# First stage of a decoder trunk: all low halves of the weights on VectorE, and the residual as one VectorE pass per tile

## The chip, the cores and the metric

The kernel runs on one core of a Trainium2 chip. The core has TensorE (PE, matmuls into PSUM), VectorE (DVE), ScalarE (ACT) and GpSimd (POOL), and queues of DMA transfers that SyncE (SP), ScalarE and GpSimd issue. The metric is the device time of one execution in microseconds, lower is better. Line numbers L... are those of the kernel before, except where a text speaks of the changed kernel.

## The reference

One decoder layer over 512 tokens of width 1024. What the change touches is at its start: the input LayerNorm, the projection to `v`, and the residual.

```python
x = layer_norm(x, ln_in_g, ln_in_b)
...
z = jnp.einsum('bsd,de->bse', x, w_in) + b_in
u_a, v_a, x_b, gate_b, q_c, merge = jnp.split(z, SPLIT_POINTS, axis=-1)
o_a = spatial_gating(jax.nn.gelu(u_a), jax.nn.gelu(v_a), ln_v_g, ln_v_b, w_s, b_s)
...
x = layer_norm(ALPHA * x + m, ln1_g[l], ln1_b[l])
f = hierarchical_moe(x, ...)
x = layer_norm(ALPHA * x + f, ln2_g[l], ln2_b[l])
```

`spatial_gating` normalises `v`, mixes the 128 positions of each chunk by a causal matrix for each of 8 channel groups, and multiplies by `u`. `m` is the mixer's output, which ends in `+ b_o`.

## The kernel before, in words

**Precision.** Each float32 matrix that goes into a matmul is split into a high half, rounded to the matmul's type by a cast, and a low half, the source minus the high half. A product is three matmul passes: high times high, and the two mixed ones. The helper `split` (L81) does the cast on ScalarE and the subtraction on VectorE. Inside the stage for `v`, the helper `split_w` (L290) does it for the weights, and takes the engine of the subtraction as an argument.

**Tiles.** The 512 tokens are four tiles `xts_[0]` to `xts_[3]` of 128x1024, called x0 to x3 here (in the order of instructions they are x_103 to x_106). The weights for `v` are four loads `raws[0]` to `raws[3]`, each split in two pieces of 128x1024, so `split_w` is called eight times. Five of these subtract on GpSimd (pieces (0,0), (1,0), (2,0), (2,1), (3,0)), three on VectorE.

**The stage for v.** For each token tile t: LayerNorm in place on VectorE (statistics, a scalar-tensor pass with the mean, a chain of eight operations on one column for the reciprocal root, L124 to L135, and a second scalar-tensor pass, L158), eight transposes on TensorE into two PSUM tiles `aux`, and their split: four casts on ScalarE and four subtractions on VectorE (L82, L83, `hl<-aux`, 128x256 each). The cast of the second half of an `aux` tile waits for the subtraction of the first half. Then two outputs of 24 matmuls of 512 columns, called p00, p01, p10 ... p31 after tile and half. `vsplit` (L327) puts the transposes of the next token tile behind the eighth matmul of the second output. `vout` (L304) adds the bias on VectorE and applies GELU on ScalarE, and `vnorm` (L309) normalises a `v` tile on VectorE.

**The residual.** `residual(t)` (L318) turns a token tile into ALPHA * x + b_o: in place, one ScalarE pass and one GpSimd addition. A DMA on GpSimd's queue stores it to `xr_d`, which is read some 500 us later.

**The u loop** (L390) follows: four steps of two channels each. A channel is 24 matmuls for `u` (`ztile`, L199), GELU, four matmuls that mix `v` by the masked matrix `wst` (L403), and the gating on VectorE (L406, L410), whose product is split again. The weights of a step are one load `raw` of 1 MB, split in two pieces (L82 and L83, `hl<-raw`). The two buffers of these loads are first those of `raws[2]` and `raws[3]`: the load for the first step waits until both subtractions of `raws[2]` are done.

**What sets the order.** Each engine works through its queue in order. Inside the stage for `v` (between `man.enter_context` and `man.close()`) the order is that of the code. What lies behind, the u loop among it, is placed by a scheduler of the framework, which can lift instructions into gaps of that order: so the first u weights' split, the small operations on `lt` (L545 to L559), and the eight passes on `bs` (L388) come between instructions of the stage.

Of the kernel before, what the change touches and what calls it, by code (L numbers as in the profile page):

```python
# [9 lines left out]
F32 = mybir.dt.float32  # L10
# [3 lines left out]
AF = mybir.ActivationFunctionType  # L14
ALU = mybir.AluOpType
# [21 lines left out]
ALPHA = 2.0 ** 0.25  # L37
# [16 lines left out]
def trunk(ctx, tc, x, mem, rows, cols, wz, wkv, pac, pb8, pb2, wax, ws, wo, wr, br, we, out):  # L54
    nc = tc.nc
    pe, dve, act, pool, sp = nc.tensor, nc.vector, nc.scalar, nc.gpsimd, nc.sync
# [12 lines left out]
    def mmps():  # L69
        return psm.tile([P, 512], F32, name="mm")  # L70
# [4 lines left out]
    def bcast(eng, pool_, r, name):  # L75
        t = pool_.tile([P, D], F32, name=name)
        i = ROWS.index(r)
        eng.dma_start(t, rows[i:i + 1, :].to_broadcast([P, D]))
        return t

    def split(hi, lo, src):  # L81
        act.copy(hi, src)  # L82
        dve.tensor_tensor(lo, src, hi.bitcast(F32), op=ALU.subtract)  # L83
# [76 lines left out]
    def layer_norm(dst, src, g, b, eps=EPS):  # L160
        ln_end(dst, ln_begin(dst, src, g), b, eps)
# [7 lines left out]
    def cc(i):  # L169
        return col[:, i:i + 1]  # L170
# [77 lines left out]
    with ExitStack() as st_a:  # L248
# [35 lines left out]
        bo = bcast(sp, s0, "b_o", "bo")  # L284
# [2 lines left out]
        sp.dma_start(wst, ws)  # L287
        wv = {}

        def split_w(i, h, eng):  # L290
            t_ = (op_ if i < 2 else hlp).tile([P, 2, 2, 512], F32R, name="o" if i < 2 else "hl")
            src = raws[i][:, 2 * h:2 * h + 2, :]
            act.copy(t_[:, 0], src)  # L293
            eng.tensor_tensor(t_[:, 1], src, t_[:, 0].bitcast(F32), op=ALU.subtract)
            wv[i, h] = t_

        def vmm(t, n, ps, lo, hi):
# [15 lines left out]
        def vfull(t, n):  # L313
            ps = mmps()
            vmm(t, n, ps, 0, 24)
            return ps

        def residual(t):  # L318
            xr = xts_[t]
            act.activation(xr, xr, AF.Copy, scale=ALPHA)  # L320
            pool.tensor_tensor(xr, xr, bo, op=ALU.add)
            pool.dma_start(xr_d[t * P:(t + 1) * P, :], xr)

        def transx(t):
            transpose_split(xts_[t], dsth(t, 0), dsth(t, 1))

        def vsplit(t, n, next_t):  # L327
# [10 lines left out]
                                                         op0=ALU.subtract, op1=ALU.mult) for c in x0h])  # L338
        for c in x0h:
            dve.scalar_tensor_tensor(xts_[0][:, c], xts_[0][:, c], rstd, bi[:, c], op0=ALU.mult, op1=ALU.add)  # L340
        split_w(0, 0, pool)
        transx(0)
        split_w(0, 1, dve)
        split_w(1, 0, pool)
        split_w(1, 1, dve)
        p00 = vfull(0, 0)
        layer_norm(xts_[1], xts_[1], gi, bi)
        split_w(2, 0, pool)
        split_w(2, 1, pool)
        split_w(3, 0, pool)  # L350
        split_w(3, 1, dve)
        p01 = vsplit(0, 1, 1)
        pool.affine_select(wst, wst, pattern=[[0, 8], [1, P]], compare_op=ALU.is_ge, fill=0.0,
                           base=0, channel_multiplier=-1)
# [2 lines left out]
        vout(0, 1, p01)  # L357
        p10 = vfull(1, 0)
        ln_end(xts_[2], ln, bi)
        residual(0)  # L360
        p11 = vsplit(1, 1, 2)
        vout(1, 0, p10)
        ln = ln_begin(xts_[3], xts_[3], gi)
        vout(1, 1, p11)
        p20 = vfull(2, 0)
        ln_end(xts_[3], ln, bi)
        residual(1)
        p21 = vsplit(2, 1, 3)
        vnorm(0)
        vout(2, 0, p20)  # L370
        p30 = vfull(3, 0)
        vout(2, 1, p21)
        vnorm(1)
        residual(2)
        p31 = vfull(3, 1)
        vout(3, 0, p30)
        residual(3)
        vnorm(2)
        last = [vout(3, 1, p31), vnorm(NT - 1)]
        man.close()  # L380
# [1 line left out]
        for i in range(2):  # L382
# [3 lines left out]
            for g in range(4 * i, 4 * i + 4):  # L386
                bg = bs[:, g * P:(g + 1) * P]
                dve.scalar_tensor_tensor(bg, ps[:, (g % 4) * P:(g % 4 + 1) * P], cc(C_VB + g), bg,  # L388
                                         op0=ALU.mult, op1=ALU.add)
        for d2 in range(4):  # L390
            with ExitStack() as after:
                for i in last if d2 else ():
                    after.enter_context(tc.issue_after(i.ins))
                w = zunit(256)
            for c in range(2):
                g = 2 * d2 + c
                ps = mmps()
                ztile(ps, w, c)
                u = sa.tile([P, T], F32, name="u", bufs=2)
                act.activation(u, ps, AF.Gelu_apprx_tanh, bias=cc(C_U + g))  # L400
                pv = auxps()
                for ch in range(NT):
                    pe.matmul(pv[:, ch * P:(ch + 1) * P], lhsT=v[:, ch, g * P:(g + 1) * P],  # L403
                              rhs=wst[:, g, :], start=True, stop=True)
                s = sa.tile([P, T], F32, name="s", bufs=2)
                dve.scalar_tensor_tensor(s.rearrange("p (c t) -> p c t", t=P),  # L406
                                         pv.rearrange("p (c t) -> p c t", t=P), cc(C_VG + g),
                                         bs[:, None, g * P:(g + 1) * P].to_broadcast([P, NT, P]),
                                         op0=ALU.mult, op1=ALU.add)
                dve.tensor_tensor(s, s, u, op=ALU.mult)  # L410
                split(oa(0, g), oa(1, g), s)

    y[0] = yp.tile([P, KD, T], F32, name="y")

# [5 lines left out]
    with ExitStack() as sc_stack:  # L420
# [15 lines left out]
        for h in range(CH):  # L436
# [19 lines left out]
            for et in range(2):  # L456
# [5 lines left out]
                                         op0=ALU.add, op1=ALU.subtract)  # L462
# [3 lines left out]
            for tp in range(2):  # L466
                ps = auxps()
                for t in (2 * tp, 2 * tp + 1):
                    for et in range(2):
# [6 lines left out]
                                  op0=ALU.mult)  # L476
# [87 lines left out]
    with tc.tile_pool(name="sb", bufs=1, reuse_waits="tile") as sb:  # L564
        ob = o_tiles()
        for hp in range(NH // 2):
# [4 lines left out]
            for c in range(2):  # L571
                h = 2 * hp + c
# [4 lines left out]
                                  op0=ALU.mult, op1=ALU.add)  # L577
# [22 lines left out]
            for c in range(2):  # L600
                h = 2 * hp + c
# [629 lines left out]
    for b in range(nb):  # L1231
# [65 lines left out]
        h = gate_h(pu, gw, c)  # L1297
# [51 lines left out]
    h = gate_h(pu, gw, c)  # L1349
# [73 lines left out]
    with tc.If(n_extra > 0):  # L1423
# [4 lines left out]
        for j in range(NEXTRA):  # L1428
# [14 lines left out]
            h = gate_h(up_mm(b), blk["gwx"], col_)  # L1443
# [80 lines left out]
```

## Time and profile before

| | us |
|---|---|
| runs shown | 942.83, 945.6, 1786.38; median 945.6 |
| the profiled execution | 940.93 |
| its span | 939.1 |
| TensorE busy | 880.2 (94%) |
| VectorE busy | 600.0 (64%) |
| ScalarE busy | 452.8 (48%) |
| GpSimd busy | 116.0 (12%) |

The stage for `v` and the first channel of the u loop lie in the first 92 us of the span. A timeline's row has the start, the duration (of a merged row: from the first start to the last end), the engine, the line, the operation, the tiles written and read, the shapes and the count; in brackets stands how long the engine idled ahead of it, and what ended that. [...]

### The profile page before, as it was taken

Reading aid. Unit: us, or ns where it says so; the run is one execution under the profiler, and the core shown is the slowest. Engines: PE = TensorE matmul, PEld = TensorE weight load, DVE = VectorE, ACT = ScalarE, POOL = GpSimd, SP = SyncE. Lnnn points to the kernel's source line nnn. Section 1 sums busy time; section 2 is a strip of 40 time slices with the busy share of each in tenths; the row PEclk is TensorE's granted clock in tenths of the full one; section 3 lists DMA queues with packets and bytes.
Section 4 is the critical chain, followed back from the end, with each engine's and each line's share of the span. In section 5 each row is a group of like instructions: output and inputs, shape, how many; then the busy total and the mean of one; then the engine's idle time right before and its main releaser. Section 6 shows DMA issues by size and latency. Waiting matters only on the chain. (4 is left out here: it accounts for less than half of the span.)

```text
span 939.1 us, 11191 instructions
## 1 busy us (share of the span) xinstructions
PE 880.2 (94%) x4260; PEld 733.2 (78%) x4260; DVE 600.0 (64%) x1011; ACT 452.8 (48%) x632; POOL 116.0 (12%) x95
## 2 busy tenths in 40 slices
PE   4798999999999999999999999999998889999990
PEld 3686888889988888888878888788877678888880
DVE  6988546324545543335667856666189987689966
ACT  4333342224434442223696686633124656678851
POOL 4322000000000100000000000000000123233843
PEclk9898999999999999999999999999999999999995
DMA  9406222332323333212214322238663888799573
GB/s 344 175 23 226 88 90 91 111 112 95 130 90 127 125 134 112 90 57 101 90 57 146 113 77 100 92 101 312 282 244 138 274 317 283 245 295 401 166 181 106
DMA packets 29867, 148.88 MB, mean 159 GB/s; under 512 B 5538, under 2 KB 5794, under 8 KB 16497
## 3 DMA queue, kind: packets, MB, share of 16 engines
q1 hardware_dynamic: 21312, 128.81, 37.6%
q0 software_dynamic: 7056, 17.12, 7.0%
q10 hardware_dynamic: 1440, 2.19, 0.7%
q8 instruction: 35, 0.57, 0.3%
q14 instruction: 24, 0.19, 0.1%
HBM read 138.33 MB, written 18.35 MB: 167 GB/s over the span
## 5 line engine op out<-in xcount | busy, mean ns | idle before, releaser
L109 PE MATMUL mm<-hl 128*128 128x512 f32 x1440 | 336.2, 392 | 0.0
L109 PEld LDWEIGHTS mm<-hl 128*128 128x128 f32 x1440 | 270.9, 189 | 56.3 <-DVE bnst L114 0.2
L83 DVE TENSOR_TENSOR hl<-raw,hl 128x1024 fp32r<-128x1024 f32 (+1 forms) x117 | 137.7, 1181 | 135.3 <-ACT hl L82 134.7
L82 ACT CAST hl<-raw 128x1024 fp32r<-128x1024 f32 (+1 forms) x117 | 117.6, 1015 | 133.0 <-PE mm L109 121.2
L109 PE MATMUL mm<-o,hl 128*128 128x512 f32 x624 | 142.9, 389 | 1.1 <-ACT o L82 1.1
L109 PEld LDWEIGHTS mm<-o,hl 128*128 128x128 f32 x624 | 117.0, 188 | 25.8 <-ACT o L82 1.5
L109 PE MATMUL mm<-hl,xs 128*128 128x512 f32 x432 | 107.5, 404 | 0.5 <-DVE xs L83 0.5
L109 PEld LDWEIGHTS mm<-hl,xs 128*128 128x128 f32 x432 | 81.0, 191 | 19.5 <-DVE xs L83 1.1
L691 DVE TENSOR_TENSOR hl<-o,hl 128x1024 fp32r<-128x1024 f32 (+1 forms) x52 | 57.8, 1143 | 2.6 <-ACT hl L685 2.6
L1142 PE MATMUL mm<-hl,hT 128*128 128x512 f32 x196 | 50.6, 404 | 0.6 <-DVE hT L83 0.6
L1006 POOL DMA_INDIRECT xg<-x_d,ixg x1 | 1.1, 1089 | 400.9 <-DVE rtl L1065 400.9
L685 ACT CAST hl<-o 128x1024 fp32r<-128x1024 f32 x48 | 48.0, 1051 | 1.7 <-PE mm L1142 1.7
L1142 PEld LDWEIGHTS mm<-hl,hT 128*128 128x128 f32 x196 | 35.6, 189 | 8.4 <-DVE hT L83 1.1
L222 ACT ACTIVATE gate<-mm,col 128x512 f32<-128x512 f32 x24 | 16.5, 688 | 39.7 <-PE mm L109 39.6
L1131 DVE TENSOR_TENSOR hl<-raw,hl 128x1024 fp32r<-128x1024 f32 x26 | 30.7, 1223 | 4.3 <-PE mm L109 2.0
L1122 ACT CAST hl<-raw 128x1024 fp32r<-128x1024 f32 x32 | 31.9, 1050 | 0.0
L525 POOL MEMSET zero<- 128x1024 f32 x1 | 1.0, 953 | 240.9 <-PE mm L109 240.9
L301 PE MATMUL mm<-o,hl 128*128 128x512 f32 x96 | 26.1, 432 | 1.8 <-ACT o L293 1.8
L109 PE MATMUL mm<-memT,hl 128*128 128x256 f32 x192 | 27.3, 286 | 0.2 <-ACT memT L82 0.2
L109 PE MATMUL mm<-hl,yh 128*128 128x512 f32 x96 | 27.0, 429 | 0.0
L733 ACT COPY x1T<-aux 128x512 f32<-128x512 f32 x8 | 4.7, 587 | 44.0 <-PE aux L732 24.0
L109 PEld LDWEIGHTS mm<-memT,hl 128*128 128x128 f32 x192 | 24.9, 191 | 0.9 <-ACT memT L82 0.4
(325 smaller groups left out, 1200.6 us busy)
## 6 DMA issues: line engine op xcount, KB each, us to landing
raw<-in_wz_dram SPq DMA_DIRECT2D x32, 1024.0 KB, 4.8
o<-in_we_dram SPq DMA_DIRECT2D x24, 1024.0 KB, 7.2
raw<-in_we_dram SPq DMA_DIRECT2D x16, 1024.0 KB, 6.8
raw<-in_pac_dram SPq DMA_DIRECT2D x8, 1024.0 KB, 4.7
raw<-in_wkv_dram SPq DMA_DIRECT2D x8, 1024.0 KB, 4.8
rawx<-in_we_dram SPq DMA_DIRECT2D x8, 1024.0 KB, 5.4
raw<-in_pb_dram SPq DMA_DIRECT2D x4, 1024.0 KB, 4.9
raw<-in_wo_dram SPq DMA_DIRECT2D x4, 1024.0 KB, 4.8
```

What stands on the lines that cost most here:

```text
L82: act.copy(hi, src)
L83: dve.tensor_tensor(lo, src, hi.bitcast(F32), op=ALU.subtract)
L109: pe.matmul(ps, lhsT=a(sa_), rhs=b(sb_), start=first and i == 0, stop=last and i == 2)
L222: act.activation(store[j], ps, AF.Sigmoid, bias=cc(C_M + br_i * 8 + j))
L301: pe.matmul(ps, lhsT=xT(k, slice(t * P, (t + 1) * P))(sx), rhs=wv[2 * n + k // 4, k // 2 % 2][:, sw, k % 2, :], start=i == 0, stop=i == 23)
L685: act.copy(t[:, 0], raws[key, i // 2][:, (i % 2) * 1024:(i % 2 + 1) * 1024])
L691: (eng or dve).tensor_tensor(t[:, 1, c0:c1], src[:, c0:c1], t[:, 0, c0:c1].bitcast(F32), op=ALU.subtract)
L733: act.copy(x1T.rearrange("p k n -> p (k n)"), ps)
L1006: pool.indirect_dma_start(out=xg, out_offset=None, in_=x1_d[:, :], in_offset=bass.IndirectOffsetOnAxis(ap=ix[:, b:b + 1], axis=0), bounds_ ...
L1122: act.copy(dnh[key][:, :, n * 512:(n + 1) * 512], dn_half(key, n))
L1131: eng.tensor_tensor(dnl[key][n], dn_half(key, n), dnh[key][:, :, ns].bitcast(F32), op=ALU.subtract)
L1142: pe.matmul(ps, lhsT=hT[:, sa_, f, :], rhs=dn[sb_][:, f, :], start=i + f == 0, stop=i + f == 3)
```

## The change

`split_w` loses its engine argument and calls `split`, so all eight low halves of the weights are subtracted on VectorE. `residual(t)` becomes one scalar-tensor pass on VectorE (x * ALPHA + b_o, in place, 128x1024); the store stays on GpSimd's queue. The four calls of `residual` leave the stage for `v`, and stand behind the second channel of each step of the u loop in the code.

```diff
-        def split_w(i, h, eng):
+        def split_w(i, h):
             t_ = (op_ if i < 2 else hlp).tile([P, 2, 2, 512], F32R, name="o" if i < 2 else "hl")
             src = raws[i][:, 2 * h:2 * h + 2, :]
-            act.copy(t_[:, 0], src)
-            eng.tensor_tensor(t_[:, 1], src, t_[:, 0].bitcast(F32), op=ALU.subtract)
+            split(t_[:, 0], t_[:, 1], src)
             wv[i, h] = t_
...
         def residual(t):
             xr = xts_[t]
-            act.activation(xr, xr, AF.Copy, scale=ALPHA)
-            pool.tensor_tensor(xr, xr, bo, op=ALU.add)
+            dve.scalar_tensor_tensor(xr, xr, ALPHA, bo, op0=ALU.mult, op1=ALU.add)
             pool.dma_start(xr_d[t * P:(t + 1) * P, :], xr)
...
-        split_w(0, 0, pool)
+        split_w(0, 0)
         transx(0)
-        split_w(0, 1, dve)
-        split_w(1, 0, pool)
-        split_w(1, 1, dve)
+        split_w(0, 1)
+        split_w(1, 0)
+        split_w(1, 1)
         p00 = vfull(0, 0)
         layer_norm(xts_[1], xts_[1], gi, bi)
-        split_w(2, 0, pool)
-        split_w(2, 1, pool)
-        split_w(3, 0, pool)
-        split_w(3, 1, dve)
+        split_w(2, 0)
+        split_w(2, 1)
+        split_w(3, 0)
+        split_w(3, 1)
...
         ln_end(xts_[2], ln, bi)
-        residual(0)
...
-        residual(1)
...
-        residual(2)
...
-        residual(3)
...
                 split(oa(0, g), oa(1, g), s)
+            residual(d2)
```

The order of VectorE's queue at three places follows; `x_103` is x0, `x_104` x1, `x_105` x2. First, from the last passes of x0's LayerNorm to the low halves of `raws[0]` and `raws[1]` (`o`), before:

```order
L135 SCALAR_TENSOR_TENSOR lnr_147<-lnt_148,lnr_147 128x1
L340 SCALAR_TENSOR_TENSOR x_103<-x_103,lnr_147,bi 128x256 x4
L83 TENSOR_TENSOR hl<-aux,hl 128x2x128 x4
L294 TENSOR_TENSOR o<-o 128x1024
L294 TENSOR_TENSOR o<-hl,o 128x1024
```

and after the change:

```order
L135 SCALAR_TENSOR_TENSOR lnr_147<-lnt_148,lnr_147 128x1
L338 SCALAR_TENSOR_TENSOR x_103<-x_103,lnr_147,bi 128x256 x4
L83 TENSOR_TENSOR o<-o 128x1024
L83 TENSOR_TENSOR hl<-aux,hl 128x2x128 x4
L83 TENSOR_TENSOR o<-o 128x1024
L83 TENSOR_TENSOR o<-hl,o 128x1024 x2
```

The low half of piece (0,0) came from GpSimd and now stands ahead of the four subtractions of x0's transposed tiles; the one of (1,0) has joined the row `x2`.

Second, from the end of x1's LayerNorm to the first bias addition of `v` (L306 before, L305 after), before:

```order
L133 SCALAR_TENSOR_TENSOR lnt_228<-lnt_228 128x1
L135 SCALAR_TENSOR_TENSOR lnr_227<-lnt_228,lnr_227 128x1
L158 SCALAR_TENSOR_TENSOR x_104<-x_104,lnr_227,bi 128x1024
L294 TENSOR_TENSOR hl<-raw,hl 128x1024
L83 TENSOR_TENSOR hl<-aux,hl 128x2x128 x4
L306 TENSOR_TENSOR y<-mm,bv 128x512
L114 BN_STATS bnst<-x_105 128x6 x2
```

and after the change:

```order
L133 SCALAR_TENSOR_TENSOR lnt_228<-lnt_228 128x1
L135 SCALAR_TENSOR_TENSOR lnr_227<-lnt_228,lnr_227 128x1
L158 SCALAR_TENSOR_TENSOR x_104<-x_104,lnr_227,bi 128x1024
L83 TENSOR_TENSOR hl<-raw,hl 128x1024 x4
L83 TENSOR_TENSOR hl<-aux,hl 128x2x128
L319 SCALAR_TENSOR_TENSOR x_103<-x_103,bo 128x1024
L83 TENSOR_TENSOR hl<-aux,hl 128x2x128 x2
L319 SCALAR_TENSOR_TENSOR x_104<-x_104,bo 128x1024
L83 TENSOR_TENSOR hl<-aux,hl 128x2x128
L305 TENSOR_TENSOR y<-mm,bv 128x512
L114 BN_STATS bnst<-x_105 128x6 x2
```

In place of one low half (`hl<-raw`) four stand behind x1's last pass, and the residual passes of x0 and x1 (L319) lie between the subtractions of x1's transposed tiles. The scheduler has lifted the residual from the u loop to here; those of x2 and x3 lie in the same place of their tiles, behind the first subtraction.

Third, x2's LayerNorm from its pass with the mean, before:

```order
L153 SCALAR_TENSOR_TENSOR x_105<-x_105,bnmv,gi 128x1024
L306 TENSOR_TENSOR y<-mm,bv 128x512
L124 TENSOR_SCALAR lnv_329<-bnmv 128x1
L548 TENSOR_SCALAR lt<-lt 128x10
L126 TENSOR_SCALAR lnr_330<-lnv_329 128x1
L549 RECIPROCAL lt<-lt 128x10
L129 SCALAR_TENSOR_TENSOR lnt_331<-lnr_330,lnv_329 128x1
```

and after the change:

```order
L153 SCALAR_TENSOR_TENSOR x_105<-x_105,bnmv,gi 128x1024
L305 TENSOR_TENSOR y<-mm,bv 128x512
L124 TENSOR_SCALAR lnv_329<-bnmv 128x1
L83 TENSOR_TENSOR hl<-raw,hl 128x1024
L126 TENSOR_SCALAR lnr_330<-lnv_329 128x1
L543 TENSOR_SCALAR lt<-lt 128x10
L129 SCALAR_TENSOR_TENSOR lnt_331<-lnr_330,lnv_329 128x1
L544 RECIPROCAL lt<-lt 128x10
```

The low half of the first piece of the first u weights (`hl<-raw`), which stood behind x2's LayerNorm, now stands inside it. Of the passes on `bs`, three have moved from behind the `v` bias addition of the last output to ahead of it. On GpSimd's queue the store of x0's residual is now ahead of the mask on `wst`. TensorE's queue is the same but for two matmuls of the first u step, which moved ahead of the last of the four mixing matmuls.

## Rows read from the trace of the kernel before

**Rows 1.** The page, busy tenths of the span in 40 slices, TensorE

```profile
PE   4798999999999999999999999999998889999990
```

**Rows 2.** Timeline of TensorE: start us, us, engine, line, operation, tiles, count [idle before <-releaser]

```profile
15.26 8.10 PE L301 MATMUL mm<-o,hl 128*128 128x512 f32 x22 [1.76 <-ACT o L293]
...
30.66 1.97 PE L187 MATMUL aux<-ident,x 128*128 128x128 f32 x8 [5.49 <-DVE x L158]
...
37.26 5.60 PE L301 MATMUL mm<-o,hl 128*128 128x512 f32 x24
...
44.52 1.03 PE L187 MATMUL aux<-ident,x 128*128 128x128 f32 x8
...
83.89 0.77 PE L403 MATMUL aux<-wst,y 128*128 128x128 f32 x2 [3.69 <-DVE y L311]
...
84.31 7.70 PE L109 MATMUL mm<-hl 128*128 128x512 f32 x22
```

**Rows 3.** Timeline of VectorE, 12 to 32 us

```profile
12.24 0.42 DVE L83 TENSOR_TENSOR hl<-aux,hl 128x256 fp32r<-128x256 f32 x1 [0.44 <-ACT hl L82]
...
17.13 2.65 DVE L294 TENSOR_TENSOR o<-hl,o 128x1024 fp32r<-128x1024 f32 x1 [0.67 <-ACT o L293]
...
21.26 1.86 DVE L153 SCALAR_TENSOR_TENSOR x<-x,bnmv,gi 128x1024 f32<-128x1024 f32 x1
...
23.41 1.98 DVE L129 SCALAR_TENSOR_TENSOR lnt<-lnr,lnv 128x1 f32<-128x1 f32 x1
...
25.43 2.26 DVE L133 SCALAR_TENSOR_TENSOR lnt<-lnt 128x1 f32<-128x1 f32 x1
...
28.56 2.04 DVE L158 SCALAR_TENSOR_TENSOR x<-x,lnr,bi 128x1024 f32<-128x1024 f32 x1
...
30.52 1.21 DVE L294 TENSOR_TENSOR hl<-raw,hl 128x1024 fp32r<-128x1024 f32 x1
```

**Rows 4.** Timeline of GpSimd, 9 to 92 us

```profile
11.88 2.36 POOL L294 TENSOR_TENSOR o<-o 128x1024 fp32r<-128x1024 f32 x1 [9.32 <-ACT o L293]
...
19.31 8.36 POOL L294 TENSOR_TENSOR hl<-raw,hl 128x1024 fp32r<-128x1024 f32 x3 [0.61 <-ACT hl L293]
...
73.27 2.88 POOL L321 TENSOR_TENSOR x<-x,bo 128x1024 f32<-128x1024 f32 x1 [3.35 <-ACT x L320]
```

**Rows 5.** Timeline of VectorE, 34 to 84 us

```profile
34.61 0.68 DVE L306 TENSOR_TENSOR y<-mm,bv 128x512 f32<-128x512 f32 x1
...
40.24 1.28 DVE L158 SCALAR_TENSOR_TENSOR x<-x,lnr,bi 128x1024 f32<-128x1024 f32 x1
...
41.44 3.18 DVE L554 SCALAR_TENSOR_TENSOR lt<-lt 128x10 f32<-128x10 f32 x5
...
59.75 1.28 DVE L114 BATCH_NORM_STATS2 bnst<-y 128x6 f32<-128x512 f32 x2
...
66.82 2.27 DVE L129 SCALAR_TENSOR_TENSOR lnt<-lnr,lnv 128x1 f32<-128x1 f32 x1
...
72.68 1.21 DVE L83 TENSOR_TENSOR hl<-raw,hl 128x1024 fp32r<-128x1024 f32 x1
...
73.80 0.20 DVE L116 BATCH_NORM_AGGREGATE bnmv<-bnst 128x2 f32<-128x12 f32 x1
...
74.42 1.74 DVE L129 SCALAR_TENSOR_TENSOR lnt<-lnr,lnv 128x1 f32<-128x1 f32 x1
...
82.93 0.81 DVE L311 TENSOR_SCALAR y<-y,bnmv,lnr 128x1024 f32<-128x1024 f32 x1
```

**Rows 6.** Stretches of 1 us: its length, busy us (count) of each engine, granted clock, DMA

```profile
28.00:29.00 1.00, 0.00 (x0) 0.00 (x0) 0.90 (x4) 0.00 (x0) 0.58 (x1) 0.54 1.05 418
...
34.00:35.00 1.00, 1.00 (x4) 0.74 (x4) 0.73 (x2) 0.98 (x2) 0.00 (x0) 0.55 0.93 393
...
82.00:83.00 1.00, 0.00 (x0) 0.00 (x0) 0.82 (x6) 1.00 (x2) 0.00 (x0) 0.85 0.96 307
```

**Rows 7.** Operations on the tiles named raw, 0 to 140 us: their loads' landing

```profile
DMA to landing us min/median/max: 4.7/4.8/13.2
```

## The prediction

> **What bounds the kernel now.** I began with the busy slices: TensorE (PE) is at nine tenths or more in nearly every slice after the first three [rows 1]. So only something that shortens PE's own queue counts, and the change touches nothing behind the first 140 us. PE's timeline of that stretch [rows 2] has two holes, both ended by VectorE (DVE): 5.49 us until the normalised token tile x1 can be transposed (at 30.66), and 3.69 us until the last normalised v tile, from `vnorm(3)`, is there (at 83.89).
>
> DVE's timeline then shows why it is late [rows 3]. A low half of 128x1024 takes 1.21 us on DVE alone (at 30.52), but 2.65 at 17.13; a scalar-tensor pass of 1.28 us takes 1.86 and 2.04; two operations on one column, 0.22 and 0.16 when alone, take 1.98 and 2.26. GpSimd (POOL) runs its tensor-tensor work in the same stretches [rows 4]: its block of three low halves ends at 27.67, and the second long column operation at 27.69. The same happens in the residual: at 41.44 five small operations take 3.18, at 66.82 and 74.42 one takes 2.27 and 1.74 [rows 5]; POOL's last addition ends at 76.15, the DVE operation at 76.16.
>
> Each hole also costs clock. The granted clock is at half (1.2 GHz) from 28.0, 2.9 us behind the last matmul, and back just before 35, 4.2 us after PE restarted at 30.66; it falls again past 82, in the second hole [rows 6]. In PE's rows 24 matmuls take 5.60 at 2.4 GHz (0.233 each), but 22 behind the second hole take 7.70, 2.6 more than 22 x 0.233; I estimate 0.43 for one at 1.2 GHz, which makes thirteen of the 22 slow, 5.6 us from 84.31 on; eight transposes take 1.97 behind the first hole and 1.03 elsewhere [rows 2].
>
> [...]
>
> **The change, part by part.** All times are us from the span's start.
>
> *DVE's account.* Gone with POOL's five low halves: 2.65-1.21 = 1.44, 1.86-1.28 = 0.58, 1.98-0.22 = 1.76, 2.26-0.16 = 2.10, 2.04-1.28 = 0.76, together 6.6 [rows 3]. Gone with its four additions: 3.18 less about 1.0 for five small operations (they start 0.2 apart) = 2.2, 2.27-0.22 = 2.05, 1.74-0.22 = 1.52, together 5.8 [rows 5]. Added: five low halves at 1.12 (start to start, 72.68 to 73.80) = 5.6, four residual passes at 1.20 (40.24 to 41.44, the same shape and operands) = 4.8 [rows 5]. So DVE ends 2.0 us lighter: 12.4 against 10.4. The gain on PE is another number, because work moves to other places. I lay it out hole by hole.
>
> *x0.* The first low half now stands ahead of x0's four subtractions. ScalarE's cast released POOL's half at 11.88 [rows 4], so on DVE it will run from about 11.85, and the subtraction that began at 12.24 [rows 3] begins at 12.98. ScalarE's next cast waits for that subtraction, and the chain through cast and subtraction to the second weight cast moves by 0.74. PE restarts at 16.0 where it did at 15.26 [rows 2], and p00 ends, by its unchanged 8.10, at 24.1; p01's first eight matmuls at 26.0. Cost 0.74.
>
> *x1.* Behind x0 DVE does three low halves and starts x1's normalisation at 19.35 (before, 19.71). Without 0.58+1.76+2.10 of stalls it lasts 5.7, so x1 is ready at 25.1, and the last pass has no stall either. PE wants it at 26.0: the hole of 5.5 us closes and the clock stays up. Even if 0.9 us of a stall remained, PE would not wait.
>
> *x1's split.* DVE now holds four low halves (to 29.5), and the residuals of x0 and x1 between the subtractions of x1's transposed tiles, so this list ends at 29.5 + 4 x 0.4 + 2 x 1.2 = 33.5. PE waits for low halves in p01 (ends 30.6; before, p10 began at 37.26 [rows 2]), then runs p10 to 36.1 and p11's first eight to 37.9. At this point PE is over 6 us ahead.
>
> *x2, the new wait.* DVE isn't ahead by that much: its first bias addition of v comes at 33.5 in place of 34.61. From there to x2's last pass was 5.63 (34.61 to 40.24) [rows 5]; the low half of the first u weights, which stood behind it, now stands inside this chain: +1.12. So x2 is ready at 33.5+5.63+1.12+1.28 = 41.5, no earlier than before (40.24+1.28 = 41.52). PE idles from 37.9, 3.6 us. The clock fell after 2.9 us last time, so I take it as falling: transposes at 1.97, then five matmuls at 0.43 till the clock is back 4.2 us after the restart (41.5 + 4.2 = 45.7), then eleven at 0.233. p11 ends at about 48.2, some 0.7 ahead of before. Most of the first gain is given back here.
>
> *x3.* Same DVE chain, 41.5 to x3 ready at 53.0 (x2's residual is in it); PE's p20 and eight of p21 end at 55.6, so no wait. PE stays 0.7 ahead to the end of p31. x3's residual lies between its subtractions and costs DVE what it was ahead: `vnorm(0)` starts near 59.7, as before (59.75).
>
> *`vnorm(3)`.* From there DVE needed 24.0 us (59.75 to 82.93+0.81 = 83.74) [rows 5]. Less 2.05 and 1.52 it needs 20.4: done at 80.2. Of the eight small passes on `bs`, three more come ahead of `vnorm(2)`'s end and three fewer behind, which cancels. PE, 0.7 ahead, gets there at 79.4. The hole is 0.8 in place of 3.7, and the clock does not fall. PE's next 20 to 22 matmuls then take 0.233 each in place of 7.70/22 = 0.35 [rows 2]: the step ends at 85.2 in place of 92.0.
>
> **Sum: 6.8 us.** After that the u loop and all behind it are the same queue on a busy PE [rows 1], so I let the 6.8 us go through undiminished.
>
> *At nothing.* ScalarE loses its four residual passes; behind the cast at 11.88 PE's holes ended with DVE, not with it. POOL's removal is worth nothing in itself. Its four stores stay on POOL's queue, the first ahead of the `wst` mask, which PE wants only past 70; x0's residual pass runs near 30 and the mask follows. The residual pass lies far from the u loop: if its cover (the casts that the subtractions wait for) were gone, four passes would cost 4.8 in place of about 3.5. The passes are bounded by 1.20 and by 2.04, the stalled row.
>
> *The unseen wait.* x2's chain now waits for the first u weights. Their load used to be freed by POOL's second-to-last half; now by the half that ends near 27.4. Loads of this size landed in 4.7 to 13.2 us [rows 7]. With 4.8 the tile is there at 32.2, and its cast follows by 36; DVE wants the cast at 37.4, so 4 us of delay are free. I take the median because the queue has emptied by 30; the long one stood behind the first megabytes.
>
> **Rivals.** *The clock doesn't fall at x2.* The hole there (3.6) is barely longer than the 2.9 us after which it fell. If it holds, PE comes 2 us sooner through x2, and DVE too, since it waits for the transposes: 8.8 us, 932.1 by the profiled run's count. [...]
>
> *The u weights land late.* A landing in 13.2 puts them at 40.6, the low half at 42.8, and x2 at about 45.6: 4.1 us more of hole, which everything behind it on DVE inherits. Gain 6.8-4.1 = 2.7, 938.2. It decides from a landing past 36.
>
> *The other side, slower.* After x2 the clock stays at 1.2 GHz until x3's transposes are through: 16+24+24 matmuls at 0.43, of which five are counted, is 59 x 0.2 = 11.8 more, 945.9, slower by 5. It decides from 34 such matmuls (6.8/0.2). Against it: at both restarts with PE kept fed the clock came back within 4 to 6 us.
>
> *No effect.* If the stalls weren't POOL's, DVE would gain 10.4 us of work in this stage and PE both holes; the ends that coincide to 0.03 us leave this little room. It would cost up to 8.
>
> **How the numbers follow.** Chances: forecast 0.55, clock holds 0.2, late weights 0.15, slower 0.07, stalls not POOL's 0.03. The profiled run took 940.93, two of the three others 942.83 and 945.6, the last being their median. 940.93-6.8 = 934.1; the same off the median, 938.8. I predict the middle, 936.4. For the forecast alone 933 to 939.5; the range 930.5 to 942.5 takes in the clock that holds and the late weights, and leaves out the last two cases. A gain of 6.8 is 0.7%, and 2%, what a measurement of this kernel can tell from no change, is 18.9 us: faster 0.02, same 0.96, slower 0.02.
>
> **What would show it.** Right: no DVE row of a column operation above 0.3 us before 85; PE's transposes of x1 with no idle ahead of them, near 26; an idle of 3 to 4 us ahead of x2's transposes near 41, behind the x pass on DVE, and half clock for about 4 us; an idle under 1.5 us ahead of the last v block near 80, at full clock. Wrong: x2's hole longer than 5 us with ScalarE waiting for the u weights' load; stalls of 2 us still in DVE's rows; the u loop's steps longer than before.

## The result, and the profile after

The changed kernel took 936.53 us (median of 11 runs, 934.91 to 941.21) against 945.6. The two medians lie 9.1 us apart; the ratio from the fast runs alone (one of the eleven runs before took 1786.38 us) is 0.993, with a 95% interval of 0.9909 to 0.9951: 6.6 us, from 4.6 to 8.6. That is the number used here. Its profiled execution took 938.02 us with a span of 936.3. From here on lines are those of the kernel that a row comes from; in the changed kernel L300 is a matmul for `v`, L319 the residual pass, L351 the mask on `wst`, L310 the last pass of `vnorm`, L397 the mixing by `wst`.

The page of the changed kernel, busy time of each engine, shows GpSimd relieved of 25 us and VectorE as loaded as before (600.0):

```profile
PE 875.4 (93%) x4260; PEld 728.6 (78%) x4260; DVE 599.3 (64%) x1020; ACT 449.2 (48%) x628; POOL 90.5 (10%) x86
```

TensorE's timeline of the changed kernel answers to [rows 2]:

```profile
11.78 1.94 PE L187 MATMUL aux<-ident,x 128*128 128x128 f32 x8 [11.78 <-DVE x L338]
...
16.94 6.99 PE L300 MATMUL mm<-o,hl 128*128 128x512 f32 x22 [2.36 <-ACT o L82]
23.77 1.98 PE L300 MATMUL mm<-hl 128*128 128x512 f32 x8
26.10 1.09 PE L187 MATMUL aux<-ident,x 128*128 128x128 f32 x8 [0.35 <-DVE x L158]
...
37.21 1.98 PE L300 MATMUL mm<-hl 128*128 128x512 f32 x8
43.67 1.18 PE L187 MATMUL aux<-ident,x 128*128 128x128 f32 x8 [4.48 <-DVE lt L549]
44.50 5.46 PE L300 MATMUL mm<-hl 128*128 128x512 f32 x16
49.80 5.60 PE L300 MATMUL mm<-o,hl 128*128 128x512 f32 x24
...
80.24 1.18 PE L109 MATMUL mm<-hl 128*128 128x512 f32 x4
81.68 0.46 PE L397 MATMUL aux<-wst,y 128*128 128x128 f32 x2 [0.26 <-DVE y L310]
81.90 4.81 PE L109 MATMUL mm<-hl 128*128 128x512 f32 x20
86.55 1.05 PE L397 MATMUL aux<-wst,y 128*128 128x128 f32 x8
```

The hole ahead of x1's transposes went from 5.49 us to 0.35, and the one ahead of the last `v` block from 3.69 to 0.26. A new hole of 4.48 us stands ahead of x2's transposes. It is ended by x2's last pass (42.24 below); the row names the small operation that lies behind that pass in time.

VectorE's timeline, then GpSimd's, of the changed kernel, against [rows 3, 5] and [rows 4]:

```profile
30.83 1.22 DVE L319 SCALAR_TENSOR_TENSOR x<-x,bo 128x1024 f32<-128x1024 f32 x1
...
32.63 2.70 DVE L319 SCALAR_TENSOR_TENSOR x<-x,bo 128x1024 f32<-128x1024 f32 x1
...
35.59 0.67 DVE L305 TENSOR_TENSOR y<-mm,bv 128x512 f32<-128x512 f32 x1
...
39.62 1.22 DVE L83 TENSOR_TENSOR hl<-raw,hl 128x1024 fp32r<-128x1024 f32 x1
...
42.24 1.28 DVE L158 SCALAR_TENSOR_TENSOR x<-x,lnr,bi 128x1024 f32<-128x1024 f32 x1
...
61.10 1.27 DVE L114 BATCH_NORM_STATS2 bnst<-y 128x6 f32<-128x512 f32 x2
...
80.72 0.81 DVE L310 TENSOR_SCALAR y<-y,bnmv,lnr 128x1024 f32<-128x1024 f32 x1
```
```profile
32.37 0.75 POOL L320 DMA_DIRECT2D xr_d<-x  x1 [29.81 <-DVE x L319]
33.12 1.13 POOL L351 TENSOR_SCALAR_AFFINE_SELECT wst<-wst 128x1024 f32<-128x1024 f32 x1
```

No operation on one column is above 0.22 us any more. One stall is left that the prediction didn't have: x1's residual takes 2.70 us where x0's takes 1.22. GpSimd's mask runs from 33.12 to 34.25, and the pass ends 1.08 us after it, nearly its own length: it was held until the mask was done. The mask came just then because the store of x0's residual (32.37) stands ahead of it on GpSimd's queue.

The granted clock (the number ahead of the last two, 1.00 for full and 0.50 for half), in stretches of 1 us of the changed kernel:

```profile
42.00:43.00 1.00, 0.00 (x0) 0.00 (x0) 1.00 (x5) 0.00 (x0) 0.00 (x0) 1.00 0.00 0
...
44.00:45.00 1.00, 1.00 (x8) 0.98 (x7) 0.86 (x6) 0.37 (x1) 0.00 (x0) 0.74 0.06 16
45.00:46.00 1.00, 1.00 (x4) 0.73 (x3) 1.00 (x2) 0.65 (x2) 0.00 (x0) 0.50 0.00 0
46.00:47.00 1.00, 1.00 (x4) 0.81 (x3) 1.00 (x4) 0.00 (x1) 0.40 (x1) 0.50 0.00 0
47.00:48.00 1.00, 1.00 (x4) 0.77 (x4) 0.89 (x5) 0.37 (x1) 0.13 (x1) 0.55 0.31 127
48.00:49.00 1.00, 1.00 (x6) 0.84 (x5) 1.00 (x3) 0.54 (x1) 0.00 (x0) 1.00 0.97 397
```

It didn't fall in the hole (39.19 to 43.67) but behind it, near 44.5, when PE was at work again, and was at 0.50 for 3.4 us (0.52+1.00+1.00+0.90, each stretch's loss doubled).

**One measure for all kernels.** The span isn't good enough to compare single executions here. Their starts differ: VectorE's wait for `gi` was 1.9 us before and 2.9 after, so x0's transposes began at 10.71 before, and between 11.10 and 11.96 in the ten other profiles. And far behind the change, in the routing stage, two waits differ. TensorE's waits between 600 and 930 us (in total, times, longest), before and then after:

```profile
PE aux L802 <- DVE cnt L788: 3.0, 1, 3.0
...
PE mm L812 <- DVE xr L807: 1.0, 2, 0.7
```
```profile
PE aux L797 <- DVE cnt L783: 4.1, 2, 3.0
PE mm L807 <- DVE xr L802: 3.0, 2, 2.6
```

That is 3.1 us, and not the change's: two kernels below that have the changed kernel's code from the u loop on show 3.0 and 1.0 there, as before did. So I use the length of the stage in the profiled execution, from the start of x0's transposes to the start of the first block of eight mixing matmuls: 91.85-10.71 = 81.14 before, 86.55-11.78 = 74.77 after, 6.4 less. In the table it stands beside the timed ratio, for all kernels run; the last column is that ratio as us, off 944.

| kernel | stage, us | against before | ratio (95%) | us |
|---|---|---|---|---|
| before | 81.14 | | 1 | |
| after | 74.77 | -6.4 | 0.9930 (0.9909 to 0.9951) | -6.6 |
| weights only | 79.78 | -1.4 | 0.9989 (0.9968 to 1.0011) | -1.0 |
| residual only | 76.01 | -5.1 | 0.9942 (0.9922 to 0.9961) | -5.5 |
| after, with GpSimd additions | 81.54 | +0.4 | 1.0016 (0.9996 to 1.0036) | +1.5 |
| after, with GpSimd memsets | 76.11 | -5.0 | 0.9961 (0.9940 to 0.9982) | -3.7 |
| after, mask late | 74.53 | -6.6 | 0.9925 (0.9895 to 0.9954) | -7.1 |
| after, u0 behind x2 | 73.77 | -7.4 | 0.9915 (0.9882 to 0.9948) | -8.0 |
| after, residual in the u loop | 72.82 | -8.3 | 0.9907 (0.9877 to 0.9937) | -8.8 |
| after, residual in the gap | 70.45 | -10.7 | 0.9897 (0.9867 to 0.9927) | -9.7 |
| the gap, and u0 behind x2 | 69.51 | -11.6 | 0.9883 (0.9856 to 0.9909) | -11.0 |

The two columns agree within 1.4 us in every row, so what the stage gains arrives at the end.

A stage's length is that of one execution, and executions of one kernel differ by up to 8.9 us; the mean granted clock tends to be lower in the slower ones. With the mask late the eight runs go from 932.14 us (mean granted clock 0.983) to 941.00 (0.976), and the profiled one is the slowest of them; with the residual in the gap the profiled one is the fastest of six (931.27 at 0.984; the slowest 936.55 at 0.980). So where a stage's length hangs on what the clock did in it, it is shown for that execution and not for the kernel.

### The profile page after: what moved, and what is told of

Its sections match the earlier page's. It is cut to its first block, busy times and chain, and to the rows that moved or that the text cites. A ratio compares the mean times of both kernels' runs of the same rounds, so it can differ in the third digit from the quotient of the medians.

```text
span 936.3 us, 11182 instructions
## 1 busy us (share of the span) xinstructions
PE 875.4 (93%) x4260; PEld 728.6 (78%) x4260; DVE 599.3 (64%) x1020; ACT 449.2 (48%) x628; POOL 90.5 (10%) x86
## 5 line engine op out<-in xcount | busy, mean ns | idle before, releaser
L109 PE MATMUL mm<-hl 128*128 128x512 f32 x1440 | 333.8, 390 | 0.0
L83 DVE TENSOR_TENSOR hl<-raw,hl 128x1024 fp32r<-128x1024 f32 (+1 forms) x121 | 142.4, 1183 | 135.4 <-ACT hl L82 134.9
L82 ACT CAST hl<-raw 128x1024 fp32r<-128x1024 f32 (+1 forms) x121 | 121.6, 1016 | 130.2 <-PE mm L109 118.1
L109 PEld LDWEIGHTS mm<-o,hl 128*128 128x128 f32 x624 | 117.1, 188 | 25.8 <-ACT o L82 1.5
L300 PE MATMUL mm<-o,hl 128*128 128x512 f32 x96 | 25.1, 419 | 2.4 <-ACT o L82 2.4
L300 PE MATMUL mm<-hl 128*128 128x512 f32 x96 | 25.1, 413 | 0.4 <-DVE hl L83 0.4
L300 PEld LDWEIGHTS mm<-o,hl 128*128 128x128 f32 x96 | 19.2, 204 | 7.3 <-ACT o L82 3.1
```

The lines of the kernel that those rows point to most:

```text
L109: pe.matmul(ps, lhsT=a(sa_), rhs=b(sb_), start=first and i == 0, stop=last and i == 2)
L300: pe.matmul(ps, lhsT=xT(k, slice(t * P, (t + 1) * P))(sx), rhs=wv[2 * n + k // 4, k // 2 % 2][:, sw, k % 2, :], start=i == 0, stop=i == 23)
```

## The experiments

My theory was the prediction's: GpSimd's work holds VectorE, VectorE's in-order queue ends PE's holes, and the holes cost clock besides. The rivals: the gain comes from one half of the change alone; the stalls aren't GpSimd's, and the gain comes from shorter queues; and, of the hole at x2, that the clock and not VectorE sets the time.

**The two halves of the change, each alone.** The first is before with the low halves on VectorE:

```diff
-            eng.tensor_tensor(t_[:, 1], src, t_[:, 0].bitcast(F32), op=ALU.subtract)
+            dve.tensor_tensor(t_[:, 1], src, t_[:, 0].bitcast(F32), op=ALU.subtract)
```

> The kernel before with all eight low halves of the weights on VectorE, the residual left on ScalarE and GpSimd. Theory (two separate gains): the hole of 5.5 us ahead of x1's transposes closes, but the stalls of the residual stay (2.2, 2.05 and 1.52 us), so vnorm(3) still ends late: a hole of 2 to 4 us ahead of the last v block, with the clock falling behind it. Gain 1.5 to 4.5 us, under the 6.6 of the whole change. Rival (the weights are the whole gain, the residual is only along): the ratio equals that of the whole change, 0.993, and the hole ahead of the last v block is under 1 us.

The second is before with the residual as one VectorE pass, in the u loop's code:

```diff
-            act.activation(xr, xr, AF.Copy, scale=ALPHA)
-            pool.tensor_tensor(xr, xr, bo, op=ALU.add)
+            dve.scalar_tensor_tensor(xr, xr, ALPHA, bo, op0=ALU.mult, op1=ALU.add)
...
-        residual(0)
...
                 split(oa(0, g), oa(1, g), s)
+            residual(d2)
```

> The kernel before with the residual as one VectorE pass behind the u steps, the five low halves left on GpSimd. Theory: the hole ahead of x1's transposes stays at 5 to 6 us with its half clock, since GpSimd's block of three still stalls VectorE; the hole ahead of the last v block shrinks from 3.7 to about 0.5 us because 3.6 us of stalls behind it are gone, and the clock there stays at full. Gain 4 to 6 us, more than the weights alone. Rival (the four added passes cost VectorE what the stalls gave back, 4.8 against 5.8): gain under 2 us, hole at the end over 2.5 us.

Weights alone gave 1.0 us in the timed runs, which is under the expected 1.5 to 4.5 and not clear of nothing (0.9968 to 1.0011); the residual alone gave 5.5, in its range. Their sum is close to the 6.6 measured, within intervals of 2 us each. TensorE's timeline of weights only, and one row of its VectorE:

```profile
26.54 1.04 PE L187 MATMUL aux<-ident,x 128*128 128x128 f32 x8
...
43.83 1.94 PE L187 MATMUL aux<-ident,x 128*128 128x128 f32 x8 [4.46 <-DVE lt L554]
...
84.62 0.77 PE L403 MATMUL aux<-wst,y 128*128 128x128 f32 x2 [3.68 <-DVE y L311]
```
```profile
39.42 2.30 DVE L135 SCALAR_TENSOR_TENSOR lnr<-lnt,lnr 128x1 f32<-128x1 f32 x1
```

and of residual only:

```profile
32.49 1.97 PE L187 MATMUL aux<-ident,x 128*128 128x128 f32 x8 [5.33 <-DVE x L158]
...
82.83 0.46 PE L398 MATMUL aux<-wst,y 128*128 128x128 f32 x2 [0.25 <-DVE y L311]
```

Each half closes its own hole: the weights x1's, the residual that of `vnorm(3)`. The closing of x1's hole, the larger of the two, is worth only about 1 us, since x2's hole opens in the same run and the one at `vnorm(3)` still waits on VectorE. There x2's hole has another cause than in the changed kernel: GpSimd's first residual addition (39.36 to 41.70) holds the one-column operation shown, and that sits in x2's chain. Closing the last hole has no later one behind it, and gives 5. The residual-only execution also has a stall that before lacks: a low half on GpSimd (11.98 to 14.55) held x0's last passes (the four took 3.76, 1.67 before). Counted from x0's transposes, x1's came 0.9 us later than before, so its stage may understate the residual's part.

**GpSimd's work put back, with nobody waiting for it.** Behind the mask of the changed kernel, four additions into a tile that is never read; and, in a second kernel, ten memsets of it, about as long in all:

```diff
+        scr = sa.tile([P, D], F32, name="scr")
+        for _ in range(4):
+            pool.tensor_tensor(scr, gi, bo, op=ALU.add)
```
```diff
+        scr = sa.tile([P, D], F32, name="scr")
+        for _ in range(10):
+            pool.memset(scr, 0.0)
```

> The changed kernel with four additions of 128x1024 on GpSimd behind the mask, of two constant tiles into a scratch tile that nobody reads: 9.4 us of GpSimd work that reads SBUF and that nothing waits for. Theory (VectorE passes with two SBUF inputs stand still while GpSimd reads SBUF): between 34 and 46 rows of VectorE stretch to 2 us and more, x2 is ready 4 to 8 us later, the hole ahead of x2's transposes grows from 4.5 to 9 or more, and the kernel takes 4 to 8 us more than the changed one. Rival (the stalls of before came from the data that VectorE waited for): nothing waits for these additions, so no change.

> The changed kernel with ten memsets of 128x1024 on GpSimd in the same place, also about 9.5 us of GpSimd work, that write SBUF and read none. Theory (it is GpSimd's reading that excludes VectorE): no row of VectorE stretches but the one by the mask, ratio as the changed kernel's, 0.993. Rival (any GpSimd work holds VectorE up, or its writes do): stretched rows as with the additions, 4 to 8 us slower.

The additions took back all of the gain (1.0016, about 8 us over the changed kernel). VectorE's, GpSimd's and TensorE's rows with the additions:

```profile
32.21 5.05 DVE L319 SCALAR_TENSOR_TENSOR x<-x,bo 128x1024 f32<-128x1024 f32 x1
...
40.86 3.29 DVE L153 SCALAR_TENSOR_TENSOR x<-x,bnmv,gi 128x1024 f32<-128x1024 f32 x1
```
```profile
33.77 2.40 POOL L355 TENSOR_TENSOR scr<-gi,bo 128x1024 f32<-128x1024 f32 x1
```
```profile
50.27 1.94 PE L187 MATMUL aux<-ident,x 128*128 128x128 f32 x8 [9.11 <-DVE lt L552]
```

x1's residual is now held through the mask and the first addition: that ends at 36.17, the pass at 37.26, again 1.09 behind. x2's pass with the mean and the first u weights' low half (2.70 in place of 1.22) are held in the same way, and x2's hole doubles to 9.11 us. This puts the stalls down to GpSimd's instructions: nothing waits for their data.

With the memsets VectorE's wide passes keep their time, but some small operations don't:

```profile
37.55 0.87 DVE L543 TENSOR_SCALAR lt<-col 128x10 f32<-128x10 f32 x1
...
38.54 1.28 DVE L153 SCALAR_TENSOR_TENSOR x<-x,bnmv,gi 128x1024 f32<-128x1024 f32 x1
...
41.59 0.87 DVE L546 TENSOR_SCALAR lt<-lt 128x10 f32<-128x10 f32 x1
```
```profile
36.41 9.06 POOL L355 MEMSET scr<- 128x1024 f32 x9
```

One memset is 1.007 us (9.06/9), so the second ends at 38.42 and the sixth at 42.45. L543 ends at 38.42, L546 at 42.46, and both took 0.87 where they take 0.15 and 0.16 in the changed kernel: two stalls of 0.7, which lengthen x2's chain by 1.4 and the stage by 1.34 (76.11 against 74.77). The timed ratio is 2.9 us above the changed kernel's, with intervals that overlap; that part is unclear. So these memsets weren't free for VectorE. The pass with two inputs in SBUF kept its 1.28, the two operations of the form tensor-scalar on ten columns took 0.87, and the one on one column (L124) kept 0.14. What decides between them isn't shown. My theory had the memsets at nothing, and failed in this.

**The hole at x2: two causes taken away, one at a time.** First the mask, held back until x3's LayerNorm is done (a one-column copy of x3 on GpSimd ahead of it):

```diff
-        pool.affine_select(wst, wst, pattern=[[0, 8], [1, P]], compare_op=ALU.is_ge, fill=0.0,
-                           base=0, channel_multiplier=-1)
...
         ln_end(xts_[3], ln, bi)
+        late = sa.tile([P, 1], F32, name="late")
+        pool.tensor_copy(late, xts_[3][:, 0:1])
+        pool.affine_select(wst, wst, pattern=[[0, 8], [1, P]], compare_op=ALU.is_ge, fill=0.0,
+                           base=0, channel_multiplier=-1)
```

> The changed kernel with the mask of wst on GpSimd made to wait for x3's LayerNorm (by a copy of one column ahead of it), so that it no longer runs at 33.1. Theory: the residual pass of x1 took 2.70 us there because the mask held it; it takes 1.22 now, x2 is ready 1.5 us earlier, the hole ahead of x2's transposes is 3.0 instead of 4.5 us, and 1 to 2 us are gained over the changed kernel (ratio 0.991 to 0.992). If the clock holds in the shorter hole, 1.8 more. Rival (the stores that GpSimd issues at 32.4 and 35.7 stalled the pass): it still takes over 2 us and x2's hole stays at 4.5.

Second the low half of the first u weights, issued behind x2's LayerNorm (`ln_end` returns its last pass):

```diff
-        ln_end(xts_[2], ln, bi)
+        x2_done = ln_end(xts_[2], ln, bi)
...
-                for i in last if d2 else ():
+                for i in last if d2 else (x2_done,):
```

> The changed kernel with the low half of the first u weights queued behind x2's LayerNorm. Theory: x2 is ready 1.1 us earlier, the hole ahead of x2's transposes is 3.4 instead of 4.5; but the half then stands ahead of the subtractions of x2's transposed tiles, and holds p20 for about as long: gain 0 to 1 us over the changed kernel, less than the mask's. Rival (the half in the chain costs its 1.1 us in full): p20 starts 1.1 us earlier. No waits for the load in either.

With the mask late, x1's residual takes 1.22, though the store ahead of it still runs (at 32.44), so it was the mask and not the store that held the pass. x2's hole shrinks by 1.4 us, as the theory says, but the profiled execution's stage gains only 0.2, and the timed ratio (0.9925 against 0.9930) is too wide to tell 0 from the 1 to 2 us expected. VectorE, TensorE and clock with the mask late:

```profile
32.70 1.22 DVE L319 SCALAR_TENSOR_TENSOR x<-x,bo 128x1024 f32<-128x1024 f32 x1
```
```profile
42.26 1.94 PE L187 MATMUL aux<-ident,x 128*128 128x128 f32 x8 [3.08 <-DVE lt L551]
```
```profile
41.00:42.00 1.00, 0.00 (x0) 0.00 (x0) 1.00 (x1) 0.00 (x0) 0.00 (x0) 0.72 0.00 0
42.00:43.00 1.00, 0.74 (x4) 0.77 (x5) 0.86 (x6) 0.00 (x0) 0.00 (x0) 0.50 0.00 0
...
48.00:49.00 1.00, 1.00 (x6) 0.78 (x5) 0.96 (x3) 0.25 (x1) 0.00 (x0) 0.86 0.10 37
```

Here the clock fell inside the hole, near 41.4, and came back only near 48.3: 6.8 us at 0.50 where the changed kernel had 3.4. The transposes take 1.94 and the 16 matmuls 5.96; p20 begins at 49.65 against 49.80. In this execution the clock ate the shorter hole, so both theories had a part: VectorE's queue sets the hole, and the clock how much of it is worth anything. With u0 behind x2 the hole is 3.48 and the low clock lasts 3.4 us as in the changed kernel. There p20 begins 1.0 us earlier (37.04 us behind x0's transposes, against 38.02), and the 1.0 us reaches the stage's end. That was the rival: I had expected the half to hold p20 for about as long from its new place. By the timed runs (0.9915) this gain isn't clear of nothing.

**The residual elsewhere.** First, in the u loop indeed: the changed kernel's code has it there, but the scheduler lifts it into the stage. Held behind the last `vnorm`:

```diff
-            residual(d2)
+            with tc.issue_after(last[1].ins):
+                residual(d2)
```

> The changed kernel with the four residual passes queued behind vnorm(3), where the code has them. Theory: x2 is ready 2.4 us (two passes) and 1.5 us (the mask, which now runs at 29 and stretches a low half by 1.1 instead) earlier, the hole ahead of x2's transposes falls from 4.5 to under 2 us, the clock stays at full, p20 starts 3 to 4 us earlier; the passes cost nothing in the u loop, where VectorE waits. vnorm(3) ends 3 to 4 us earlier. Gain over the changed kernel 3 to 4 us, ratio 0.989. Rival (VectorE has no room in the first u steps either): the first u steps become longer than 6.35 us and the ratio stays 0.993.

Second, those of x0 to x2 and the mask behind x3's LayerNorm, where VectorE was idle for 3.46 us in the changed kernel (ahead of x3's first subtraction), and x3's in the last u step:

```diff
-        pool.affine_select(wst, wst, pattern=[[0, 8], [1, P]], compare_op=ALU.is_ge, fill=0.0,
-                           base=0, channel_multiplier=-1)
...
         ln_end(xts_[3], ln, bi)
+        for t in range(3):
+            residual(t)
+        pool.affine_select(wst, wst, pattern=[[0, 8], [1, P]], compare_op=ALU.is_ge, fill=0.0,
+                           base=0, channel_multiplier=-1)
...
-            residual(d2)
+            if d2 == 3:
+                with tc.issue_after(last[1].ins):
+                    residual(3)
```

> The changed kernel with the passes of x0, x1 and x2 behind x3's LayerNorm, where VectorE idles for 3.5 us until x3's transposes, the mask behind their stores, and the pass of x3 in the last u step. Theory: as with the passes in the u loop, the hole ahead of x2's transposes falls under 1.5 us and the clock holds; here no low half meets the mask. p20 starts 4 us earlier; the three passes end before x3's transposes are through. Gain over the changed kernel 3 to 5 us, ratio 0.988 to 0.990. Rival (VectorE is no longer ahead at x3 once PE is faster, so the passes hold x3's split): p30 waits 1 to 3 us and the gain is under 2 us.

Third, the second with u0 behind x2's LayerNorm as well:

> This is the kernel with the residuals of x0 to x2 and the mask behind x3's layer norm, and in addition the half of the first u block's weights is issued behind x2's layer norm. Theory (VectorE's in-order queue sets the hole ahead of x2's transposes, and that half stands in x2's chain for 1.2 us): the hole shrinks from 1.87 us to about 0.7 us, all later steps of the stage come about 1.2 us earlier or less, where the u block then has to wait for its weights; ratio to the kernel before 0.987 to 0.990. Rival (the clock sets the time, since it did not fall in the kernel without this edit): the hole shrinks but the stage's end is moved by less than 0.3 us, and the ratio is the same as that kernel's 0.9897 within its interval.

TensorE's rows of x2's transposes in the three, and the clock in the second:

```profile
41.40 1.94 PE L187 MATMUL aux<-ident,x 128*128 128x128 f32 x8 [2.31 <-DVE lt L550]
```
```profile
26.04 1.09 PE L187 MATMUL aux<-ident,x 128*128 128x128 f32 x8 [2.04 <-DVE x L158]
...
40.90 1.06 PE L187 MATMUL aux<-ident,x 128*128 128x128 f32 x8 [1.87 <-DVE lt L553]
41.72 3.90 PE L300 MATMUL mm<-hl 128*128 128x512 f32 x16
```
```profile
39.24 1.06 PE L187 MATMUL aux<-ident,x 128*128 128x128 f32 x8 [0.85 <-DVE x L158]
```
```profile
40.00:41.00 1.00, 0.10 (x1) 0.13 (x2) 0.96 (x3) 0.00 (x0) 0.00 (x0) 1.00 0.00 0
```

With the residual in the u loop no store stands ahead of the mask, which now runs at 28.67 and stretches one of x1's four low halves by 0.9; the hole is still 2.31 us and the clock falls, where I had expected under 2 and full clock: the stage gains 2.0 us over the changed kernel and not 3 to 4. With it in the gap, neither residual nor mask touches x2's chain: the hole is 1.87 us (under 1.5 was expected), the clock stays at 1.00, and the 16 matmuls take 3.90. That is the step from -8.3 to -10.7, as far as one execution of each shows it: 1.6 of the 2.4 us lie between the start of x2's transposes and p20, where the clock fell in one and held in the other. x3's first subtraction comes behind the three passes, and no wait of TensorE follows. Moving u0 as well takes another 1 us off the hole and 0.9 off the stage. This last kernel, 932.48 us (931.48 to 935.48), is the fastest of all, and its interval lies below that of the changed kernel, touching it at 0.9909. The order of the last three among themselves isn't settled by the timed runs, whose intervals overlap; the stage's lengths order their profiled executions only.

## Why the prediction was right, and where its steps were off

Times of the changed kernel are given here less 1.07 us, its later start. The total was right (6.8 predicted, 6.6 timed, 6.4 in the stage), and so was its shape: x1's hole closes, most of that is given back at x2, the last hole closes and its clock with it.

- *x0, 0.74 us.* PE restarted at 15.87; 16.0 was predicted. But "by its unchanged 8.10" failed: the 22 matmuls took 6.99, and between 5.30 and 8.12 over all kernels. In the changed kernel three or four of them fall in each us up to 21, and six behind; the granted clock reads 1.00 all through, so what set their pace isn't shown. The delay reached nothing, because x1's transposes wait for VectorE anyway: in the kernel with 5.30 they begin 14.31 us after x0's, in the changed kernel 14.32.
- *x1.* Ready predicted at 25.1, transposes at 25.03. Right. That its stalls would go whole was my estimate, and they did: its two passes take 1.28 each (1.86 and 2.04 before), and none of its operations on one column over 0.22 (1.98 and 2.26).
- *The mask ("at nothing").* This step failed. The prediction saw that the store of x0's residual would stand ahead of the mask, and asked only who needs the mask. The mask also cost what VectorE ran beside it: x1's residual was held for 1.48 us (2.70 in place of 1.22), and the first bias addition began at 34.52, 1.0 late (the rest of that list took 3.6 and not 4.0). The price stood in the rows of before. The prediction put the 0.76 of x1's last pass (28.56 to 30.60) down to GpSimd's low halves, but these end at 27.67; what ran beside the pass was the mask, and the pass ends 1.08 us behind it:

```profile
28.42 1.10 POOL L353 TENSOR_SCALAR_AFFINE_SELECT wst<-wst 128x1024 f32<-128x1024 f32 x1 [0.75 <-DMA wst<-in_ws_dram]
```

So the 0.76 was the mask's, not the low halves'. The mask had only moved, behind the store, from x1's last pass to x1's residual.
- *x2.* The new hole is there, with its cause: the half of u0 takes 1.13 in the chain, start to start (1.12 predicted). It is 4.48 in place of 3.6 us, outside the 3 to 4 named as the sign; the mask's 1.48, less the shorter list, explains it, and with the mask late the hole is 3.08. The clock's part was mis-sized the other way: half clock was predicted in the hole and for 4.2 us behind the restart, but it came 0.8 us behind the restart and lasted 3.4, so that eight transposes took 1.18 and not 1.97. p20 began at 48.73 (49.05 before), so PE was 0.3 ahead there and not 0.7. (The prediction's own 48.2 for p11's end is 1.0 ahead of before's 49.21; it carried on with 0.7.) This is the rival "clock holds" in half. The traces give the clock as a share of full alone, so where the prediction has 2.4 and 1.2 GHz, 1.00 and 0.50 are what was measured. The 0.43 for a matmul at half clock is in the trace of before: with the clock at 0.50 three of them start at 85.74, 86.17 and 86.59.
- *Late u weights.* The loads landed in 4.6 to 12.4, 4.7 in the median, and no wait for them shows. Right to be a rival only.
- *x3 and `vnorm(3)`.* No wait at x3. From `vnorm(0)` to the end of the last pass VectorE needed 20.43 us (61.10 to 81.53 in its rows); 20.4 was predicted. The hole is 0.26 and not 0.8, since PE was 0.4 less ahead and two more matmuls (0.47) stood in front of it. The clock held, the next 20 matmuls took 4.81 and ended at 85.64; 85.2 was predicted. Right.
- *VectorE's account.* Its busy time fell by 0.7 us (600.0 to 599.3) and not by 2.0; the mask's 1.48 on x1's residual is about the difference.
- *Undiminished to the end.* Right by the timed runs and by the table; the two profiled executions alone (2.8 us in the spans) would have spoken against it.
- *Stalls not GpSimd's, no effect.* Ruled out by the additions. *Slower by the clock*: the clock came back after 3.4 or 6.8 us, wherever it was read that far.

That the median fell within 0.2 us of the predicted number is partly luck: the mask's 1.48 us on one side, the hidden 0.74 and the milder clock on the other, cancelled; and the prediction counted from the middle of two runs of before, while the changed kernel's own runs lie 6.3 us apart.

## What to carry to other kernels

Work taken off GpSimd was worth the stalls it had caused on VectorE only where VectorE's queue ended a wait of the bound engine; follow the queue from hole to hole, because a hole closed early can be given back at the next one (x1's, 5.49 us long and closed alone, gained 1.0 us in the timed runs, which isn't clear of nothing). An instruction that "nobody waits for" can still have a price where it runs (1.48 us for the mask): look what VectorE does beside it, and at what releases it, as with the mask behind a store. Place passes with a far due time by hand in a gap of the engine that has one; a scheduler that lifts them into the first free slot put them into the chain here, and undoing that, with the mask moved too, brought the gain from 6.6 to 11.0 us in the timed runs.

## What the runs showed of the hardware

- A wide VectorE pass with two inputs in SBUF that met a low half, a mask or an addition of GpSimd was, in the cases read here, held until that instruction's end and then took nearly its full length: it ended 1.08 or 1.09 us behind, at a length of 1.22 or 1.28 (behind the mask and the addition in the kernels above; before, behind a low half, 18.70 to 19.78, and behind the mask, 29.52 to 30.60). With the additions put back, the mask and the first of them, back to back, held it through both (5.05 us). In the changed kernel the row of the pass begins 0.49 us ahead of the mask's, and it was held all the same.
- GpSimd was held too: before, its addition that began at 54.50, inside VectorE's last pass on x3 (54.36 to 55.65), took 3.39 us and ended 2.24 behind that pass; another, at 66.68, took 2.38 in all.
- In the kernel with the memsets, GpSimd's memset held two tensor-scalar operations on ten columns of VectorE (0.87 in place of 0.15 and 0.16), though it left one on one column (0.14) and wide passes of two inputs alone (1.28).
- After a last matmul near 39 us the clock fell at 41.4, 41.4, 42.8 and 44.5 in kernels whose holes were 2.31, 3.08, 3.48 and 4.48 us, and not at all with 1.87, nor with x1's hole of 2.04 in that same kernel; it was at 0.50 for 6.8 us with 3.08 and for 3.4 with the others. Three further kernels had holes of 4.46, 5.87 and 9.11 us and a low clock for 3.4, 6.8 and at least 5.7 us (still at 0.50 at 52). Each is one execution, and whether another of the same kernel falls at the same place isn't shown. So the price of a hole wasn't a smooth function of its length in these executions: a hole 1.4 us shorter gained 0.2 us, and one 0.4 us shorter than 2.31 gained the whole clock back.
